# A two-layer transformer kernel: the opening's transform units moved sooner, its fill order rewritten, and several stage joints changed

## The chip, the cores and the metric

The kernel runs on one core of a Trainium2 chip. The metric is the device time of one execution in microseconds (us). The kernel before took 1864.59 us, the median of 3 runs (1861.81 to 1866.3). Engine names are those of the profile: PE is TensorE (PEld are its weight loads), DVE is VectorE, ACT is ScalarE, POOL is GpSimd and SP is SyncE.

## What is computed

The reference is a diffusion transformer of two layers, on 256 tokens of x and 256 tokens of context, model width 2048, branch width 4096. Layer 0 mixes by a two-dimensional Fourier transform in 16 groups of 256 channels; layer 1 is sliding-window attention with a sink and the context as extra keys. Both are modulated by vectors made from c (and c_ctx) by the weights ada_w.

```python
xc = ctx
for i in range(DEPTH):                       # 0: fourier, 1: attention
    shift, scale, gate = split(silu(c) @ ada_w[i] + ada_b[i], 3)
    h = rmsnorm(x, norm_g[i]) * (1 + scale) + shift
    # hc: the same of xc with c_ctx
    if kind == 0:
        u, z = split(h @ w_in, 2)            # 16 groups of 256 channels
        f = fft2(ug, axes=(tokens, channels), norm='ortho').real
        y = einsum('bngc,gcd->bngd', f, w_mix) * silu(z)
        # yc the same of hc
    else:
        q, k, v, z = split(h @ w_in)         # kc, vc from hc
        y = attend_with_sink(q, keys, values, mask) * silu(z)
    x = x + gate * (y @ w_out[i])
    xc = xc + gate_c * (yc @ w_out[i])       # layer 0 only
return rmsnorm(x, final_g)
```

The inputs and the output are float32.

## The kernel before

**Products.** Every large product is made of three matmuls on rounded parts (`mm3`, L74): high by high, high by low, low by high. So each tile has to be split first (`split`, L61): ACT casts the high part, and DVE subtracts it to get the low part. A weight tile arrives as a 1 MB "raw" tile on SP's DMA queue and is split in two halves.

**Order.** A scheduler puts the instructions of each engine in an order, by its own estimate of when they can run. The program steers it with `tc.issue_after(ins)`: what stands in that block comes after `ins`. On the chip each engine, and each queue of DMAs, then works strictly in that order, so one instruction that waits holds all behind it. Buffers come from pools; taking a tile from a full pool waits for the last reader of an old one. [...]

**The opening (L140 to L432).** The modulation weights of layer 0 (shift and scale) are 32 tiles of 1 MB, `in_awp`. `opening_step(p)`, p = 0 to 15, takes two each:

- `ada_tile` (L216) multiplies a weight tile with the conditioning on PE; after eight of them, in two steps, `ada_rows` (L221) copies rows off PSUM on ACT, and `ada_fin` turns them on PE with the identity (L228) and reduces and finishes them on DVE (L232 to L235). Shift (`sh0`) and scale (`gs0`) come in four quarters each.
- `x_split` splits the four token tiles of x for one quarter of the channels, and `dft_unit(k)` applies the token transform to channel block k, 12 matmuls, six for each of the two sequences. `evac_dft` copies the result off PSUM.
- `scale_hx(k)` multiplies by the scale (L288 ACT, L289 DVE), once the scale of that quarter is there. `fix_f0` puts the shift into column 0, the zero frequency (DVE, L239 to L245); it needs the shift of that quarter, so a product that reads column 0 comes after it.
- `fill_pe(n)` takes the next n steps of the list `fill`: the 80 projection steps of groups 0 and 1 (`u_step`: the part "m" reads columns 128 to 255, the part "p" reads columns 0 to 129 and so column 0) and of the special frequencies (`sp_step`, "s", column 0 too). Each step is one `mm3`.
- `uload` says at which step a weight tile of groups 0 and 1 (`in_wu`) is loaded. All loads share a ring of 7 raw slots, later 5 (`raw_st`, L190), and take the slot with the smallest "until".
- `load_m(g)` loads the mixing weights of group g on ACT's queue (one buffer, L354), folds and splits them, and multiplies them with the channel transform on PE (10 matmuls). load_m(0) stands in step 9.

**The groups (L448 to L526).** For each of the 16 groups the two 1 MB weight tiles (halves kh = 0 and 1 of the contraction) are folded into a difference and a sum (`fold_uh`, L132: DVE; for some of them the sum is made in place by an accumulating DMA on POOL's queue, L141), and split into eight tiles (`split_uh`). PE does 48 matmuls of the part "m", then the mix of the group before (14), then 48 of the part "p". The mix writes two tiles of `fd` to DRAM on POOL's queue (L522; the last group's go on ACT's).

**The z stage and the first output product.** Transposed x comes again in tiles `xT` on POOL's queue (L576), is modulated (L582 to L584) and multiplied with `wz`; the result gates `fd`. Then layer 0's output product runs, 32 weight tiles, and `evac0` (L639) adds x, squares on ACT (L645, L648) and adds the squares of the first blocks on DVE (L650).

**The joint to layer 1.** The sums of squares over channels are matmuls with a column of ones (L698, L700). `rsqrt` (L82) makes the norm with POOL's power (L90). Meanwhile `x1_turn` transposes the new x on PE (L690), copies it on ACT (L692), and stores it to DRAM `x1d` on ACT's queue (L693). The norm is broadcast by matmuls (L720) and copied (L721); then `h` of layer 1 is made (L756 to L760) and the key and value product starts, with the first `wkv` tile split before (one half in the last step of the product before, the other while POOL works on the power).

**The tail.** After the attention, `o1_step` multiplies the attention's output, split by `y_split`, with the second half of `w_out[1]`. Channel blocks k under 16 go to the pool `h1`, k = 16 to 19 to `act`, and the others to a pool `ys` that exists only when the attention's own pool is closed.

Of the kernel before, what the change touches and what calls it, by code (L numbers as in the profile page):

```python
# [16 lines left out]
P = 128  # L17
# [5 lines left out]
G = 16  # L23
# [5 lines left out]
def tile_dit(ctx: ExitStack, tc: tile.TileContext, a: dict, out: bass.AP):  # L29
# [29 lines left out]
    last_cast = [None]  # L59

    def split(h, l, src):  # L61
        last_cast[0] = S.copy(h, src).ins  # L62
        V.tensor_tensor(l, src, h.bitcast(F32), op=ALU.subtract)  # L63
# [15 lines left out]
    v_end = [None]  # L79

    def rsqrt(pool, src, w, tag, ahead=None):
# [3 lines left out]
        if ahead is None:  # L85
            V.tensor_scalar(v, src, 1.0 / D, EPS, op0=ALU.mult, op1=ALU.add)
        else:
            V.tensor_scalar(v, ahead, 1.0 / D, EPS, op0=ALU.mult, op1=ALU.add)
            v_end[0] = V.scalar_tensor_tensor(v, src, 1.0 / D, v, op0=ALU.mult, op1=ALU.add).ins
# [53 lines left out]

    def split_uh(v, m):
        fl = {}
        for nm, t in (("m", m), ("p", v)):
            l = wfp.tile([P, 8, 127], F32R, tag="wf", name=f"w{nm}l")
            h = wfp.tile([P, 8, 127], F32R, tag="wf", name=f"w{nm}h")
            split(h, l, t)
            fl[nm] = (h, l)  # L150
        return fl
# [14 lines left out]
    with tc.tile_pool(name="st", reuse_waits="tile", bufs=1, side="right") as st:  # L166
# [22 lines left out]
        def raw_st(src, until):  # L189
            slot = min(ring, key=lambda r: r[1])  # L190
# [58 lines left out]
        def x_split(nb):  # L249
            for s in range(2):  # L250
# [40 lines left out]

        raws, pend = {}, []
        units = {1: (), 2: (4, 5), 3: (6, 7), 4: (8, 9), 5: (10, 11), 6: (12, 13), 7: (14, 15)}

        def opening_step(p):
# [3 lines left out]
            if p in (1, 3, 5):  # L299
                x_split((p + 1) // 2)  # L300
            us_ = units.get(p, ())
            if p < 2:
# [4 lines left out]
            elif us_:  # L307
                for k in us_:
                    dft_unit(k, (0,))
            else:  # L310
                fill_pe(4)
            for i in (2 * p, 2 * p + 1):
                ada_tile(i)
            if p in uload:
                raws[uload[p]] = load_uh(*uload[p], raw_st, uhold[uload[p]])
# [8 lines left out]
            elif p > 7:  # L324
                fill_pe(4)
# [12 lines left out]
        wu = [[None, None], [None, None]]  # L338
        raws[0, 0] = fold_uh(raws[0, 0], 0, 0)
        opening_step(6)  # L340
        with tc.issue_after(rows_end[0]):
            wu[0][0] = split_uh(*raws[0, 0])
        opening_step(7)
        raws[1, 0] = fold_uh(raws[1, 0], 1, 0)
# [32 lines left out]
        ou = [{}, {}]  # L377
        parts = (("m", 128, 256), ("p", 0, 130))

        def u_step(g, nm, k):  # L380
            c0, c1 = dict(m=(128, 256), p=(0, 130))[nm]
            if k == 0:
                ou[g][nm] = psum()[0:127, 0 : 2 * (c1 - c0)].rearrange("p (s j) -> p s j", s=2)
            wh, wl = wu[g][k // 8][nm]
            h, l = hx[k]
            return mm3(ou[g][nm], wh[:, k % 8, :], wl[:, k % 8, :], h[:, :, c0:c1], l[:, :, c0:c1], k == 0, k == KT - 1)

        def sp_step(k):
            if k == 0:
                ou[0]["s"] = psum()[0:32, 0:260].rearrange("p (s j) -> p s j", s=2)  # L390
            h, l = hx[k]
            q = slice(k * 32, (k + 1) * 32)
            return mm3(ou[0]["s"], sph[:, q], spl[:, q], h[:, :, 0:130], l[:, :, 0:130], k == 0, k == KT - 1)
# [8 lines left out]
        def fill_pe(n):  # L402
            for _ in range(n):
                g, nm, k = fill.pop(0)
                with pe_next():
                    r = sp_step(k) if nm == "s" else u_step(g, nm, k)
            pe_end[0] = r

        for p in range(8, 16):
# [9 lines left out]
            if p == 9:  # L419
                with pe_next():  # L420
                    bcast_rows(rr, r_bc)
# [6 lines left out]
            for kh, q in ((0, 9), (1, 11)):  # L428
# [18 lines left out]
    for g in range(G):  # L447
        if g == 2:  # L448
            with tc.issue_after(f0_end[0]):
                w = [split_uh(*f) for f in v2]  # L450
        else:
            w = load_u(g) if g > 1 else wu[g]
# [8 lines left out]
        if g == 1:  # L461
            with tc.issue_after(f0_end[0]):
                pqh, pql, sp = load_m(g)
# [23 lines left out]
        if g == 0:  # L487
            ov = ou[0]["s"]
            S.copy(asp[0:32], ov)
            S.copy(asp[64:96], ov)  # L490
            pqh, pql, sp = m0
            asp_end = V.tensor_tensor(asp[32:64], ov, asp[0:32].bitcast(F32), op=ALU.subtract).ins
# [8 lines left out]
        split(ph, pl, oa["p"])  # L501

        def mix(g=g, mh=mh, ml=ml, ph=ph, pl=pl, pqh=pqh, pql=pql, sp=sp):
            for db in range(2):
# [17 lines left out]
                (nc.gpsimd if g < G - 1 else nc.scalar).dma_start(fd[g * 2 + db], ft.rearrange("p s j -> p (s j)"))  # L522
# [728 lines left out]
```

## Time and profile before

| | |
|---|---|
| runs, median of 3 | 1864.59 us (1861.81 to 1866.3) |
| the profiled execution | 1861.88 us |
| its span | 1859.8 us, so 2.1 us lie around it |
| instructions | 26500 |
| PE busy | 1817.1 us, 98% |
| DVE busy | 1387.8 us, 75% |
| ACT busy | 955.3 us, 51% |
| DMA | 367.42 MB, mean 198 GB/s |

The busy share of an engine is a mean over all stages. The row of forty digits shows the same share for each fortieth of the span, 46.5 us, so the opening is the first two and a half digits. The list of waits names, for one engine, the instruction that waited, what it waited for, the sum of these waits, how often, and the longest. The timeline gives the start and the duration of an instruction (or of several alike in a row, "x16"), and in brackets the idle time of its engine before it and what ended that. A matmul of float32 that is not rounded is shown as two records. "Granted clock" is the share of PE's clock that the chip allowed in that stretch.

### The profile page before, as it was taken

The page shows a single profiled execution, that of the slowest core. Times are in us where ns is not written, and L with a number is a line of the kernel's source. Part 1 is how long each engine was busy: PE and PEld are TensorE (multiplying, and loading weights), DVE is VectorE, ACT ScalarE, POOL GpSimd, SP SyncE. Part 2 cuts the span into 40 slices and gives each one's busy share as a digit, 9 for nine tenths or more (in the row PEclk, how much of TensorE's full clock was granted, in tenths as well). Part 3 has the DMA queues.
Part 4 walks back from the last instruction along what each step waited for, and adds up shares of the span by engine and source line. Part 5 has one row for each costly group of instructions (what it writes and reads, how often), then busy time and mean ns, then how long its engine had stood idle before and what let it go on. Part 6 is the DMA issues. An engine that isn't in the chain of part 4 may idle for free.

```text
span 1859.8 us, 26500 instructions
## 1 busy us (share of the span) xinstructions
PE 1817.1 (98%) x9897; PEld 1549.1 (83%) x9897; DVE 1387.8 (75%) x2770; ACT 955.3 (51%) x1660; POOL 179.4 (10%) x189
## 2 busy tenths in 40 slices
PE   6899999999999999999999999999999999999997
PEld 4579999888888888888888888888888888887886
DVE  4759888786868788588984836888878878887454
ACT  5534445432222243214222524888888888896343
POOL 0011111100000000000000001111220220300001
PEclk9999999999999999999999999999999999999999
DMA  9989888666656547654675324333333333434543
GB/s 394 418 284 246 230 237 238 225 232 231 229 219 232 210 180 271 258 217 149 227 281 218 114 91 144 128 136 125 125 115 135 136 114 136 159 137 178 187 179 136
DMA packets 76129, 367.42 MB, mean 198 GB/s; under 512 B 23200, under 2 KB 23344, under 8 KB 40928
## 3 DMA queue, kind: packets, MB, share of 16 engines
q1 hardware_dynamic: 48960, 324.57, 47.5%
q0 software_dynamic: 22320, 33.15, 7.1%
q10 hardware_dynamic: 4720, 8.00, 1.4%
q8 instruction: 78, 1.28, 0.3%
q14 instruction: 51, 0.42, 0.1%
HBM read 353.10 MB, written 12.59 MB: 197 GB/s over the span
## 4 chain that ended last, share of the span: by engine, by line
PE 79%; DMA 9%; issue 6%; DVE 3%; ACT 2%; POOL 0%; ACTq 0%; SPq 0%; POOLq 0%; DVEq 0%
PE ps L75 19%; PE ps L76 19%; PE ps L77 19%; PE ps L950 6%; PE ps L952 3%; DMA raw<-in_awp 3%; PE ps L1006 3%; DMA raw<-in_wu 3%; PE ps L1021 2%; PE ps L1020 2%; PE ps L986 2%; PE ps L987 2%; PE ps L216 1%; DMA raw<-in_adw 1%; DMA xn<-in_x 1%
## 5 line engine op out<-in xcount | busy, mean ns | idle before, releaser
L62 ACT CAST wh<-raw 128x1024 fp32r<-128x1024 f32 x333 | 349.2, 1051 | 546.3 <-PE ps L76 464.7
L63 DVE TENSOR_TENSOR wl<-raw,wh 128x1024 fp32r<-128x1024 f32 x333 | 421.3, 1267 | 232.0 <-ACT wh L62 229.2
L76 PE MATMUL ps<-act,wh 128*128 128x512 f32 x1024 | 398.2, 389 | 0.0
L75 PE MATMUL ps<-act,wh 128*128 128x512 f32 x1024 | 393.7, 389 | 0.0
L77 PE MATMUL ps<-act,wl 128*128 128x512 f32 x1024 | 392.6, 389 | 0.1
L77 PEld LDWEIGHTS ps<-act,wl 128*128 128x128 f32 x1024 | 192.2, 188 | 40.2 <-DVE wl L63 0.5
L76 PEld LDWEIGHTS ps<-act,wh 128*128 128x128 f32 x1024 | 192.2, 188 | 39.9
L75 PEld LDWEIGHTS ps<-act,wh 128*128 128x128 f32 x1024 | 192.2, 188 | 39.8
L553 DVE CUSTOM_DVE_ANT_0 raw<-raw,cb 128x512 f32<-128x512 f32 x256 | 172.7, 689 | 26.3 <-DMA raw<-in_adw 22.8
L950 PE MATMUL ps<-h,wh 128*128 128x512 f32 x512 | 186.9, 400 | 0.0
L553 DVE CUSTOM_DVE_ANT_0 junk<-raw,cb 128x512 f32<-128x512 f32 x192 | 131.9, 687 | 25.0 <-ACT cb L545 12.5
L952 PE MATMUL ps<-h,wl 128*128 128x256 f32 x512 | 138.1, 280 | 0.0
L75 PE MATMUL ps<-wh,h 128*128 128x512 f32 x320 | 124.1, 396 | 1.6 <-ACT h L757 1.6
L76 PE MATMUL ps<-wl,h 128*128 128x512 f32 x320 | 125.5, 392 | 0.0
L77 PE MATMUL ps<-wh,h 128*128 128x512 f32 x320 | 124.0, 391 | 0.0
L950 PEld LDWEIGHTS ps<-h,wh 128*128 128x128 f32 x512 | 96.1, 188 | 18.8
L988 DVE CUSTOM_DVE_ANT_0 ps<-ps,mask,nsink 128x512 f32<-128x512 f32 x128 | 92.1, 754 | 12.1 <-PE ps L987 11.2
L991 ACT ACTIVATE p<-ps,mx 128x512 f32<-128x512 f32 x128 | 87.3, 687 | 24.7 <-DVE mx L988 24.1
L952 PEld LDWEIGHTS ps<-h,wl 128*128 128x128 f32 x512 | 96.8, 189 | 1.4
L63 DVE TENSOR_TENSOR pl<-ps,ph 128x512 fp32r<-128x512 f32 x128 | 83.7, 685 | 10.0 <-ACT ph L62 8.7
L996 ACT ACTIVATE p<-p,sm 128x512 f32<-128x512 f32 x128 | 85.4, 716 | 8.2 <-DVE sm L994 8.2
L76 PE MATMUL ps<-wl,ys 128*128 128x512 f32 x212 | 83.3, 393 | 0.0
(322 smaller groups left out, 3575.4 us busy)
## 6 DMA issues: line engine op xcount, KB each, us to landing
raw<-in_wz SPq DMA_DIRECT2D x64, 1024.0 KB, 4.9
raw<-in_adw SPq DMA_DIRECT2D x64, 1024.0 KB, 4.9
raw<-in_awp SPq DMA_DIRECT2D x32, 1024.0 KB, 13.0
raw<-in_wo SPq DMA_DIRECT2D x32, 1024.0 KB, 6.1
raw<-in_wq SPq DMA_DIRECT2D x32, 1024.0 KB, 4.8
raw<-in_wu SPq DMA_DIRECT2D x32, 1016.0 KB, 7.0
raw<-in_wo1b SPq DMA_DIRECT2D x16, 1024.0 KB, 4.8
act<-in_xT POOLq DMA_DIRECT2D x32, 256.0 KB, 5.3
```

The lines of the kernel that those rows point to most:

```text
L62: last_cast[0] = S.copy(h, src).ins
L63: V.tensor_tensor(l, src, h.bitcast(F32), op=ALU.subtract)
L75: PE.matmul(o, wh, xh, start=start, stop=False)
L76: PE.matmul(o, wh, xl, start=False, stop=False)
L77: return PE.matmul(o, wl, xh, start=False, stop=stop).ins
L553: V.tensor_tensor_reduce(junk if s == 0 and i < 3 else wf, wf, cb[:, s, kq * 512 : kq * 512 + 512], 1.0, 0.0, ALU.mult, ALU.add, acc[:, i, ...
L950: PE.matmul(o[0], wh[:, q], hx1[k], start=k == 0, stop=k == KT - 1)
L952: PE.matmul(o[0][:, 0:N], wl[:, q], hx1[k][:, 0:N], start=False, stop=False)
L988: V.tensor_tensor_reduce(o, o, mask[:, tb, :], -0.125, nsink[:, i : i + 1], ALU.add, ALU.min, mx[:, tb : tb + 1])
L991: S.activation(pt[:, tb, :], so[tb], AF.Exp, bias=mx[:, tb : tb + 1], scale=-1.0, accum_out=sm[:, tb : tb + 1])
L996: S.activation(pt[:, tb, :], pt[:, tb, :], AF.Copy, scale=sm[:, tb : tb + 1])
L1006: PE.transpose(o[:, (kt * 2 + tb) * P : (kt * 2 + tb + 1) * P], pt[:, tb, c : c + P], ident)
```

## The change

The opening:

- The transform units of blocks 4 to 15 stand in steps 2 to 6 (three, two, three, two, two) instead of two in each of the steps 2 to 7. The x tiles of quarters 2 and 3 are split one sequence at a time, in steps 2, 3, 4.
- Projection steps start in step 7 (eight before the modulation tiles, four after); step 12 has none, step 14 four. The list `fill` goes in runs of four blocks, ordered by the quarter of scale and shift that they need.
- The weight tiles of groups 0 and 1 are loaded in steps 4, 6, 7 and 9 instead of 4, 6, 8 and 10; folds, splits and the closing of the pools move with them.
- The broadcast of the first norm stands in step 5, not after step 9. load_m(1) stands in step 11, not in the loop over groups.

The groups: the m halves of group 2 are split first, and its p halves after the split of group 1's p result. Group 3's loads and splits are to come after the first mix. The `fd` stores of group 14 go on ACT's queue.

The joint: the squares are kept as four sums (blocks 0 to 12, 13, 14, 15). The matmuls that sum the first two stand just ahead of the very last product of the output stage, the other two behind it, and DVE adds the four. The second half of the first `wkv` tile is split after the first `h` is made and the last squares are taken. The x1d stores go on SP's queue.

The tail: y blocks 16 to 23 go to `act`.

```diff
     def split_uh(v, m):
-        fl = {}
-        for nm, t in (("m", m), ("p", v)):
...
+        return {"m": split_part("m", m), "p": split_part("p", v)}
...
-        def raw_st(src, until):
-            slot = min(ring, key=lambda r: r[1])
+        def raw_st(src, until, slots=7):
+            slot = min(ring[:slots], key=lambda r: r[1])
...
-        def x_split(nb):
-            for s in range(2):
+        def x_split(nb, ss_=(0, 1)):
+            for s in ss_:
...
+        fill = []
+        for g, nm, k in ((0, "m", 0), (0, "p", 0), (0, "m", 4), (1, "m", 0), (1, "p", 0), (0, "p", 4), (1, "m", 4), (1, "p", 4), (0, "s", 0), (0, "s", 4), (0, "m", 8), (1, "m", 8), (0, "p", 8), (1, "p", 8), (0, "s", 8), (0, "m", 12), (1, "m", 12), (0, "p", 12), (0, "s", 12), (1, "p", 12)):
+            fill += [(g, nm, k + i) for i in range(4)]
...
-        units = {1: (), 2: (4, 5), 3: (6, 7), 4: (8, 9), 5: (10, 11), 6: (12, 13), 7: (14, 15)}
+        units = {2: (4, 5, 6), 3: (7, 8), 4: (9, 10, 11), 5: (12, 13), 6: (14, 15)}
+        fills = {7: (8, 4), 12: (0, 0), 14: (4, 0)}
...
-            if p in (1, 3, 5):
-                x_split((p + 1) // 2)
+            if p == 1:
+                x_split(1)
+            if p in (2, 4):
+                x_split(p // 2 + 1, (0,))
...
-            else:
-                fill_pe(4)
+            elif fl[0]:
+                fill_pe(fl[0])
+            if p in (3, 4):
+                x_split(p // 2 + 1, (1,))
+            if p == 5:
+                with pe_next():
+                    bcast_rows(rr, r_bc)
...
-            elif p > 7:
-                fill_pe(4)
+            elif p > 6 and fl[1]:
+                fill_pe(fl[1])
...
-        uload = {4: (0, 0), 6: (1, 0), 8: (0, 1), 10: (1, 1)}
-        uhold = {(0, 0): 5.5, (1, 0): 7.5, (0, 1): 8.9, (1, 1): 10.9}
-        for p in range(6):
+        uload = {4: (0, 0), 6: (1, 0), 7: (0, 1), 9: (1, 1)}
+        uhold = {(0, 0): 4.9, (1, 0): 6.9, (0, 1): 7.9, (1, 1): 9.9}
+        for p in range(5):
             opening_step(p)
...
-        fill = [(g, nm, k) for g in range(2) for nm in ("m", "p") for k in range(8)]
-        fill += [(0, "s", k) for k in range(8)]
-        fill += [(g, nm, k) for g in range(2) for nm in ("m", "p") for k in range(8, 12)]
-        fill += [(g, "m", k) for g in range(2) for k in range(12, 16)]
-        fill += [(0, "s", k) for k in range(8, 12)] + [(0, "p", k) for k in range(12, 16)]
-        fill += [(0, "s", k) for k in range(12, 16)] + [(1, "p", k) for k in range(12, 16)]
...
+            if p == 11:
+                with pe_next():
+                    m1 = load_m(1)
-            for kh, q in ((0, 9), (1, 11)):
+            for kh, q in ((0, 8), (1, 10)):
...
         if g == 2:
+            mix0 = ft_end[0]
             with tc.issue_after(f0_end[0]):
-                w = [split_uh(*f) for f in v2]
+                w = [{"m": split_part("m", m)} for v, m in v2]
+                with tc.issue_after(p1_end[0]), tc.issue_after(p1_end[1]):
+                    for f, (v, m) in zip(w, v2):
+                        f["p"] = split_part("p", v)
         else:
-            w = load_u(g) if g > 1 else wu[g]
+            with tc.issue_after(mix0) if g == 3 else nullcontext():
+                w = load_u(g) if g > 1 else wu[g]
...
-                (nc.gpsimd if g < G - 1 else nc.scalar).dma_start(fd[g * 2 + db], ft.rearrange("p s j -> p (s j)"))
+                (nc.gpsimd if g < G - 2 else nc.scalar).dma_start(fd[g * 2 + db], ft.rearrange("p s j -> p (s j)"))
...
-            if 0 < k < 14:
+            if 0 < k < 13:
                 V.tensor_tensor(sqs[0], sqs[0], t2, op=ALU.add)
             else:
                 sqs.append(t2)
 
+        def row_sums(i):
+            for t in range(4):
+                st_end[0] = PE.matmul(sums[0][:, i * 4 + t : i * 4 + t + 1], sqs[i][:, t * P : (t + 1) * P], ones[:, 0:1], start=True, stop=True).ins
...
+                last = i == 31 and (j, b) == (1, 7)
+                if last:
+                    sums.append(psum())
+                    with tc.issue_after(e):
+                        row_sums(0)
+                        row_sums(1)
+                with tc.issue_after(st_end[0]) if last else nullcontext():
+                    e = mm3(o[b], w[j][0][:, q], w[j][1][:, q], *yy[i, j], kg + j == 0, kg * 2 + j == NB - 1)
...
-        nc.scalar.dma_start(x1d[tb, :, c * 512 : (c + 1) * 512], t)
+        nc.sync.dma_start(x1d[tb, :, c * 512 : (c + 1) * 512], t)
...
+    for i in (2, 3):
+        row_sums(i)
+    ssum = const.tile([P, 4], F32, name="ssum")
+    V.tensor_reduce(ssum, sums[0][:, 0:16].rearrange("p (i t) -> p t i", i=4), axis=AX.X, op=ALU.add)
+    r4 = rsqrt(const, ssum, 4, "q")
...
-                with tc.issue_after(h_end[0]):
-                    w = ws_split(raw(a["wkv"][kg])) if kg else w0
+                with tc.issue_after(h_end[0]), tc.issue_after(sq_end[0]):
+                    w = ws_split(raw(a["wkv"][kg])) if kg else [w0, half_split(wr, 1)]
...
-                if 16 <= k < 20:
+                if 16 <= k < 24:
                     t = act(F32R)
...
-                while len(yh) <= min(k + 4, NB - 1) and (len(yh) < 20 or fin):
+                while len(yh) <= min(k + 4, NB - 1) and (len(yh) < 24 or fin):
```

More of the change, by code (lines that the diff above doesn't have):

```diff
@@ L142, in fold_uh, with split_part @@
         return v[:, :, 0, :], m
-    def split_uh(v, m):
-        fl = {}
-        for nm, t in (("m", m), ("p", v)):
[L147 to L151, printed above, removed]
+    def split_part(nm, t):
+        l = wfp.tile([P, 8, 127], F32R, tag="wf", name=f"w{nm}l")
+        h = wfp.tile([P, 8, 127], F32R, tag="wf", name=f"w{nm}h")
+        split(h, l, t)
+        return h, l
+    def split_uh(v, m):
+        return {"m": split_part("m", m), "p": split_part("p", v)}
     def load_u(g):
@@ L298, in opening_step @@
                 x_split(0)
-            if p in (1, 3, 5):
-                x_split((p + 1) // 2)
+            if p == 1:
+                x_split(1)
+            if p in (2, 4):
+                x_split(p // 2 + 1, (0,))
             us_ = units.get(p, ())
+            fl = fills.get(p, (4, 4))
             if p < 2:
@@ L461, in tile_dit @@
         if g == 1:
-            with tc.issue_after(f0_end[0]):
-                pqh, pql, sp = load_m(g)
+            pqh, pql, sp = m1
         elif g > 2:
@@ L489, in tile_dit @@
             S.copy(asp[0:32], ov)
[L490 removed]
+            asp_end = [S.copy(asp[64:96], ov).ins]
             pqh, pql, sp = m0
[L492 removed]
+            asp_end.append(V.tensor_tensor(asp[32:64], ov, asp[0:32].bitcast(F32), op=ALU.subtract).ins)
         mh, ml = am[g % 2]
@@ L692, in x1_turn @@
         S.copy(t, o)
-        nc.scalar.dma_start(x1d[tb, :, c * 512 : (c + 1) * 512], t)
-    sums = [psum(), psum()]
-    for t in range(4):
-        for i in range(2):
-            PE.matmul(sums[0][:, t : t + 1], sqs[i][:, t * P : (t + 1) * P], ones[:, 0:1], start=i == 0, stop=i == 1)
-    for t in range(4):
-        st_end = PE.matmul(sums[1][:, t : t + 1], sqs[2][:, t * P : (t + 1) * P], ones[:, 0:1], start=True, stop=True).ins
-    r4 = rsqrt(const, sums[1][:, 0:4], 4, "q", sums[0][:, 0:4])
-    with tc.issue_after(sq_end[0]), tc.issue_after(v_end[0]):
-        w0.append(half_split(wr, 1))
+        nc.sync.dma_start(x1d[tb, :, c * 512 : (c + 1) * 512], t)
[4 more added lines that the diff above has]
+    r4 = rsqrt(const, ssum, 4, "q")
     r4h = const.tile([P, 4], F32R, name="r4h")
@@ L708, in tile_dit @@
     r_bc1 = act()
-    with tc.issue_after(st_end):
+    with tc.issue_after(st_end[0]):
         o = psum()
```

69 lines of the change are left out of this document (34 added, 35 removed).

## The prediction

> **What bounds the kernel now.** The page first: one busy engine, and it is not full everywhere.
>
> ```profile
> span 1859.8 us, 26500 instructions
> PE 1817.1 (98%) x9897; PEld 1549.1 (83%) x9897; DVE 1387.8 (75%) x2770; ACT 955.3 (51%) x1660; POOL 179.4 (10%) x189
> PE   6899999999999999999999999999999999999997
> DMA  9989888666656547654675324333333333434543
> ```
>
> TensorE is busy for 1817.1 of 1859.8 us. The idle 42.7 us lie in the first slices (the opening), in the tail, and in a few joints. The diff leaves the number of products alone, so it can win only there, or lose by opening new gaps. The list of waits on TensorE says where the gaps are:
>
> ```profile
> PE ps L75 <- DVE dh L184: 12.9, 2, 11.6
> PE ps L216 <- DMA raw<-in_awp: 10.6, 8, 2.9
> PE ps L75 <- ACT h L757: 1.6, 1, 1.6
> PE ps L75 <- ACT mh L62: 1.5, 1, 1.5
> PE ps L76 <- DVE apl L63: 1.3, 1, 1.3
> PE ps L75 <- ACT ys L62: 0.8, 1, 0.8
> ```
>
> The start (12.9 us, for x and the transform) is not touched. The 10.6 us are waits for modulation weights in the opening. The other four are joints, each within reach of a part of the diff. The third view is busy time by stretches of the opening (columns: TensorE, its weight loads, VectorE, ScalarE, GpSimd, granted clock, DMA share, GB/s):
>
> ```profile
> 90.00:100.00 10.00, 7.84 (x64) 5.41 (x62) 5.13 (x16) 2.09 (x2) 0.00 (x0) 1.00 1.01 420
> 100.00:102.00 2.00, 0.98 (x8) 0.33 (x12) 0.00 (x0) 0.00 (x0) 0.00 (x0) 0.59 1.04 434
> 102.00:104.00 2.00, 2.00 (x16) 0.26 (x8) 0.00 (x0) 0.00 (x0) 0.00 (x0) 0.55 0.97 373
> 110.00:120.00 10.00, 9.31 (x67) 6.61 (x66) 7.23 (x24) 5.95 (x16) 3.73 (x3) 1.00 0.68 228
> ```
>
> From 10 to 100 us every window has a DMA share of 1.01 or 1.02 at 416 to 424 GB/s: a 1 MB tile every 2.49 us, and TensorE waits for it. By 110 us this is over, and TensorE is the late one. So the opening is two queues in a row: weights first, then the products that were put off. The timeline at the end of it:
>
> ```profile
> 114.22 2.46 DVE L132 TENSOR_TENSOR wm<-raw 128x1016 f32<-128x1016 f32 x2
> 114.79 1.92 PE L216 MATMUL ps<-raw,c 128*32 128x512 f32 x16
> 118.17 0.60 PE L228 MATMUL ps<-ident,rows 128*128 128x128 f32 x4
> 118.80 0.19 DVE L232 TENSOR_REDUCE sh<-ps 128x8 f32<-128x32 f32 x1 [2.12 <-PE ps L228]
> ```
>
> The last modulation tile landed at 108.56, but TensorE reaches it only at 114.79. That 6.2 us is the slack the opening's rearrangement can use.
>
> **The opening, step by step.** Transform units move from steps 2–7 to 2–6, their x tiles are split in halves, and the products of groups 0 and 1 start at step 7 instead of 8, in an order of what is ready. TensorE's own work is the same but for load_m(1), which moves in from the group loop (10 products, 1.25 us). What changes is when it is done: while weights arrive. load_m(1)'s DMA also comes ahead of the last tiles: 0.26 MB at 0.42 MB/us is 0.6 us, so I put the last landing at 108.56 + 0.6 = 109.2.
>
> Does TensorE keep up? From the tile of step 9 (about 80 us by landings) to step 15's first half I add 28.8 us from rows: 12 products of a projection 1.6, a pair of modulation tiles 1.9, a turned row 0.6, load_m(1) 1.25. So it is there at about 109, with the landing, and done with the last tile at 110.3 instead of 116.71. Behind it come 12 projection products without column 0 (1.6), the turn of the last rows (0.6), 12 more (1.6): 114.1 at most, 113.8 without the ends. Then every product left needs column 0, which is fixed by VectorE after the last rows.
>
> That fix is late next. VectorE has both folds of group 2 ahead of the last reduce in its order, and the second fold needs the second weight tile of group 2. It landed at 115.44; two tiles at 2.49 after 109.2 gives 114.2. Fold 1.21, reduce and fix 1.49 (118.80 to 120.29): 116.9. TensorE stalls about 3.1 us, where before it had no wait at this place. 36 products (4.7) and the first mix (1.75) follow: group 2's m part starts at 123.3, against 127.30.
>
> The stall costs a second time. After 1.86 us idle at 29.14–31.01 the granted clock was 0.53 and 0.62 for 4 us, and 24 products took 4.33 us where others took 3.12. After 2.94 us (98.08–101.02, the lines above) it was 0.59 and 0.55, and 16 weight products took 3.27, not 1.92. After 1.43 to 1.68 us idle it stayed 1.00. The nearest rows to 3.1 say a loss of 1.2; bounds 0 and 1.35 (3.27 − 1.92). Gain of the opening: 4.0 − 1.2 = **2.8 us**. Bounds: 7.6 if the fix costs no stall (the last pair 6.4 sooner, load_m(1) out of the loop 1.25), below nothing if load_m(1) blocks (rival 2).
>
> [...]
>
> **The weights of groups 2 and 3.** Group 2's m halves are split first and its p halves after group 1's. The reason to look: the second m half of group 2 was ready at 130.6 and used at 130.7, that of group 3 at 145.7 for 146.7. If the loop starts 4 us sooner, they must be sooner too. Group 2's was behind the GpSimd accumulate DMAs (126.15 landing, then cast 1.05 and subtract 1.21 of the p half); without that it is ready near 120. Group 3's tile is issued when a raw slot is freed by group 2's split; all that moves 3 us, I get 143 for 144. So the gain is kept, with 1 us to spare. Later groups had 1.1 to 3.4. The wait of 1.26 us at 223.36 hangs on a tile that landed at 219.93 ahead of VectorE's queue (2.33 wait there); its order of folds and splits is the same from there. It goes or stays: **+0.5**, bounds 0 and 1.3.
>
> **Stores of group 14 on ScalarE's queue.** Two issues at 0.33 us on ScalarE; GpSimd's queue can issue xT loads sooner. The 1.55 wait at 333.47 is for a cast behind L583, which waits for L582 and an xT tile that was issued at 323.93, when TensorE freed its buffer, before those stores (325.99). So 0, bounds −0.5 and +0.5.
>
> **Joint of the layers.** The lines before:
>
> ```profile
> 1032.63 1.92 PE L698 MATMUL ps<-ones,act 128*128 128x1 f32 x16 [0.49 <-DVE act L650]
> 1034.41 1.03 PE L700 MATMUL ps<-ones,act 128*128 128x1 f32 x8
> 1039.86 1.25 ACTq L693 DMA_DIRECT2D x1d<-act  x2
> 1041.15 0.59 ACT L721 COPY act<-ps 128x512 f32<-128x512 f32 x1 [0.83 <-PE ps L690]
> 1043.19 0.50 PE L75 MATMUL ps<-wh,h 128*128 128x512 f32 x1 [1.59 <-ACT h L757]
> ```
>
> Row sums are 16 records in 1.92; now there are 32 instead of 24, and 16 stand ahead of the last product. They push its end, the last evacuation and square by about 1.8: sums end at 1033.72 + 1.84 + 1.1 = 1036.7, 1.3 later than 1035.44. One reduce (0.2) is added, one VectorE step (0.16) goes. So r and its broadcast are 1.3 later. Against this, the x1d stores leave ScalarE: the copy at 1041.15 stood behind issues that ended 1041.11 (0.83 idle), and the first h behind one at 1042.25 (0.33): up to 1.0 back. The split of the second weight half leaves VectorE's gap (1.22) and comes behind h, where 24 products (5.5 us) cover it; the raw slot it frees is then some 8 us later, and the next load, before at 1036.80, has until the third tile is used to land. SP's stores wait for ScalarE's copies, and only that load is queued behind them. Sum **−0.3**, bounds −1.3 and +1.0.
>
> **Four more y tiles before the tail.** The casts for the last product wait at 1699.12 stand behind a copy at 1698.84 from the last head. With y 20–23 split early, TensorE has 24 more products (5.6 us) before it needs them. The 0.76 and 0.29 waits go: **+1.0**, bounds 0 and 1.05.
>
> **Sum.** 2.8 + 0.5 + 0 − 0.3 + 1.0 = 4.0 us. The profiled execution took 1861.88 (span 1859.8 and 2.1 around it), 2.7 below the median of 1864.59. So it becomes 1857.9, and the median 1860.6.
>
> **Rivals.**
> 1. *The gain is eaten by supply.* TensorE arrives sooner at groups 2 to 9, but folds and splits are paced by raw slots and VectorE, busy 67.0 of 70 us between 130 and 200. Slacks of 0.1 and 1.0 at the second m halves speak for it, the removed accumulate wait against it. If their times stay, the opening's 2.8 return as waits at L75: 4.0 − 2.8 = 1.2, or 1863.4.
> 2. *Slower: load_m(1) blocks TensorE in the opening.* Its tile has one buffer, so its load is issued only when VectorE has read load_m(0)'s, and VectorE now has two folds, eight scalings and the splits of cst and wsp ahead of that. Such loads took 7.34 and 11.42 us while the DMA was full. TensorE wants it at step 11, about 88 us. Read at 76, as m0's landing at 75.59 allows, it is there at 83 to 88; each microsecond later holds all that follows in order, and the ring with its five slots (12.4 us of transfers) fills up. The stall at the fix hides the first 3.1; beyond it group 2's m part starts at 120.5 + d. Slower by 3.7 needs a loss of 4.9 in the opening, d = 11.6, so VectorE reading m0 at 88 to 92. For it speaks the order, against it that the folds' weights land some two tiles sooner than before. At d = 12: opening −5.2, sum −4.0, 1868.6.
> 3. *No stall at the fix, or no clock drop.* If the second tile of group 2 lands by 111 and TensorE never stalls, the opening gives up to 7.6: sum 8.8, 1855.8. If it stalls and the clock holds, 1859.4. For the first speaks that TensorE frees slots sooner; against it the full DMA.
>    [...]
> 4. *The rearrangement does nothing*: were the opening bound by landings alone. Against it the 6.2 us between 108.56 and 114.79. Joints alone: 1.2, 1863.4, as in 1.
>
> **How the numbers follow.** Forecast 0.43; its own range is 1858.5 to 1862.6 (the joint, the wait of 1.26 and the stores at their ends). Rivals 1 and 4 0.22, rival 2 0.15, rival 3 0.20, half each way. 0.2% is 3.7 us, about what a measurement of this kernel can tell from no change, so faster begins at 1860.9. Of the forecast 0.25 lies below that; with rival 3, 0.45 faster. Same: 0.18 of the forecast and 0.18 of rivals 1 and 4, 0.36. Slower: rival 2 and 0.04 of rival 1 with the joint at its worst, 0.19. The range reaches from just under rival 3's first case to where a third of rival 2 is in, 1855.5 to 1867.5.
>
> **What would show it.** Right: the last modulation pair on TensorE at 109–111; a wait of about 3 us for a fixed column (ScalarE or VectorE f0, L244/L245 before) at 114–117 with a halved clock behind it; group 2's m part at 123–125; no wait for a wml tile until 150; first kv product at 1043.5 less the shift, no issue on ScalarE before the r_bc1 copy; no ys wait near 1699. Wrong: waits for weights of groups 2–4 of over 1 us; the DMA share below 0.9 anywhere from 20 to 100 us; a wait of over 5 us for an mh, cl or spw tile in the opening.

## The result and the profile after

The changed kernel took 1857.84 us, the median of 18 runs (1849.97 to 1861.9), against 1864.3 us for the kernel before (18 runs, 1859.45 to 1867.99): a ratio of 0.9965, 95% interval 0.9955 to 0.9974, so 6.5 us or 0.35% faster. On the chip of the first experiments the same kernel had a ratio of 0.9977 (0.9965 to 0.9988), 4.3 us. Forecast were 4.0 us (1860.6) and a range of 1855.5 to 1867.5.

The profiled execution is the fastest of the 18, 1849.97 us. It is 11.9 us below the profiled execution of before, nearly twice what the medians say. So what is seen in this one profile must not be taken for the effect of the change; the second profiles below sort the two apart.

The page of the changed kernel:

```profile
span 1848.2 us, 26508 instructions
...
PE 1813.5 (98%) x9905; PEld 1548.9 (84%) x9905; DVE 1388.9 (75%) x2769; ACT 955.3 (52%) x1660; POOL 177.2 (10%) x187
```

The list of waits on TensorE:

```profile
PE ps L75 <- DVE dh L182: 12.4, 2, 11.1
PE ps L214 <- DMA raw<-in_awp: 4.8, 5, 2.0
PE ps L75 <- DVE act L242: 2.9, 2, 2.6
...
PE ps L77 <- DVE wml L63: 0.7, 1, 0.7
...
PE ps L75 <- ACT h L776: 0.5, 1, 0.5
...
PE ps L75 <- ACT mh L62: 0.2, 1, 0.2
```

The wait for modulation weights fell from 10.6 to 4.8 us. A new one is there, 2.9 us for L242, the fixed column (2.59 of it at one place, 115.78). Another new one, 0.7 us for wml, stands at 64.72, in the first projection steps. The waits for apl (1.3) and ys (0.8) are gone, those for mh and h are 0.2 and 0.5 instead of 1.5 and 1.6. The end of the opening, in the timeline:

```profile
108.66 1.07 PE L214 MATMUL ps<-raw,c 128*32 128x512 f32 x8 [0.88 <-DMA raw<-in_awp]
...
113.60 1.22 DVE L130 TENSOR_TENSOR wm<-raw 128x1016 f32<-128x1016 f32 x1 [1.25 <-DMA raw<-in_wu]
114.74 0.18 DVE L230 TENSOR_REDUCE sh<-ps 128x8 f32<-128x32 f32 x1
...
115.78 0.39 PE L75 MATMUL ps<-act,wph 128*127 128x260 f32 x1 [2.59 <-DVE act L242]
...
120.51 0.28 PE L75 MATMUL ps<-mh,pqh 127*128 127x256 f32 x1
```

The last tile landed at 108.62 and is multiplied at 108.66. The second fold of group 2 (113.60) stands on VectorE ahead of the reduce (114.74), as read from the order, and TensorE waits 2.59 us. The first mix starts at 120.51 instead of 124.68.

Two profiled executions by place (start of the same instruction in both, us):

| | before | after | difference so far |
|---|---|---|---|
| first mix | 124.68 | 120.51 | −4.2 |
| mix of group 13 | 309.71 | 303.65 | −6.1 |
| mix of group 15 | 333.47 | 326.00 | −7.5 |
| first key and value product | 1043.19 | 1033.60 | −9.6 |
| last product's end | 1849.54 | 1838.09 | −11.5 |

### The profile page after: what moved, and what is told of

Its sections match the earlier page's. It is cut to its first block, busy times and chain, and to the rows that moved or that the text cites. A ratio compares the mean times of both kernels' runs of the same rounds, so it can differ in the third digit from the quotient of the medians.

```text
span 1848.2 us, 26508 instructions
## 1 busy us (share of the span) xinstructions
PE 1813.5 (98%) x9905; PEld 1548.9 (84%) x9905; DVE 1388.9 (75%) x2769; ACT 955.3 (52%) x1660; POOL 177.2 (10%) x187
## 4 chain that ended last, share of the span: by engine, by line
PE 87%; DMA 5%; issue 3%; DVE 3%; ACT 1%; POOL 0%; SPq 0%; POOLq 0%; ACTq 0%; DVEq 0%
PE ps L75 22%; PE ps L76 22%; PE ps L77 22%; PE ps L969 6%; PE ps L971 3%; PE ps L1025 3%; PE ps L1040 2%; PE ps L1039 2%; DMA raw<-in_awp 2%; PE ps L1005 2%; PE ps L1006 2%; DVE raw L565 1%; DMA raw<-in_adw 1%; PE ps L214 1%; DMA raw<-in_wo 1%
## 5 line engine op out<-in xcount | busy, mean ns | idle before, releaser
L969 PE MATMUL ps<-h,wh 128*128 128x512 f32 x512 | 187.2, 400 | 0.0
L75 PE MATMUL ps<-act,wph 128*127 128x260 f32 x256 | 74.2, 290 | 2.9 <-DVE act L242 2.9
```

What stands on the lines that cost most here:

```text
L75: PE.matmul(o, wh, xh, start=start, stop=False)
L969: PE.matmul(o[0], wh[:, q], hx1[k], start=k == 0, stop=k == KT - 1)
```

## The experiments

Waits and times come from each run's own profile, ratios from its timed runs against the kernel before on the same chip.

### Both kernels a second time, and the change in two parts

e1 is the kernel before and e2 the changed one, with no edit. e3 has the first part of the diff above, up to and with `p1_end` (opening and groups), the rest as before; e4 has its second part, from the `fd` line on (stores of group 14, joint, tail), the rest as before.

> The kernel before, unchanged, for a second profile. Two theories of what sets the 11.9 us between the two profiled executions (1861.88 and 1849.97) when the medians differ by 6.5. Place theory: each difference belongs to its place; the profile again has the three stretches of half clock (32 to 35, 100 to 104 and 1036 to 1039 us) and the waits of 1.3 us for apl near 223 and 1.5 us for mh near 333, and its time is within 1 us of 1862. Chance theory: stretches of half clock come and go between executions, so at least one of the three is missing or another is there, and the time differs by 1.7 us for each; the waits for apl and mh stay within 0.3 us of before.

> The changed kernel, unchanged, for a second profile. Place theory: no half clock at the joint near 1028, one stretch near 70 to 74, time near 1850. Chance theory: more stretches of half clock than the one of the first profile, and a time nearer the median of 1857.8. Both: a wait of 2.6 us for the fixed column near 113 to 116, group 2's m part at 122.5 to 124 us, no wait for apl near 217.

> The opening and the group order of the change, with the stores of group 14, the joint and the tail as before. Place theory: group 2's m part at 122.5 to 124 us, the wait for apl of 1.3 us gone (both belong to this part), so 4.2 + 1.4 = 5.6 us faster than before; the wait for mh near 327 is 1.5 us as before if the stores of group 14 removed it, and gone if the earlier groups did. Rival (supply): the opening's gain is given back by waits for weights in groups 2 to 9: under 2 us.

> The stores of group 14, the joint and the tail of the change, with the opening and groups as before. Place theory: 1.5 (mh) + 1.8 (joint of the layers) + 1.9 (tail) = 5.2 us faster than before. My prediction: 0 - 0.3 + 1.0 = 0.7 us. If the joint's gain is the clock alone, and chance, between 1.5 and 4 us by times, with the tail's 1.0 to 1.9 sure.

Measured: e1 1863.92 us, ratio 1.0007 (0.9992 to 1.0022); e2 1858.08, 0.9977 (0.9965 to 0.9988); e3 1859.52, 0.9983 (0.9971 to 0.9994); e4 1860.68, 0.9981 (0.9965 to 0.9996). So the halves are worth 3.2 and 3.5 us, together 6.7, and the whole 4.3 (2.2 to 6.5): the intervals are too wide to say whether they add. For e3 that is 1.1 to 5.4 us: the 5.6 of the place theory is just outside, a part of the supply theory's under 2 is inside. For e4 it is 0.7 to 6.5 us, which holds both the 5.2 and the 0.7: the time alone decides nothing there, and the profile has to.

The second profile of the changed kernel took 1861.01 us, 11 us more than the first. Its list of waits:

```profile
PE ps L76 <- DVE apl L63: 4.1, 6, 1.9
PE ps L75 <- DVE act L242: 3.2, 2, 2.6
...
PE ps L75 <- ACT mh L62: 1.0, 1, 1.0
```

The opening is the same, but there are six waits for apl, in mixes of groups 3 to 10, that the first profile has not. The longest, in the timeline of e2:

```profile
188.76 1.22 DVE L130 TENSOR_TENSOR wm<-raw 128x1016 f32<-128x1016 f32 x1 [3.48 <-DMA raw<-in_wu]
...
190.56 1.21 DVE L63 TENSOR_TENSOR wpl<-raw,wph 128x1016 fp32r<-128x1016 f32 x1
...
191.69 0.42 DVE L63 TENSOR_TENSOR apl<-ps,aph 127x260 fp32r<-127x260 f32 x1
...
192.16 0.39 PE L76 MATMUL ps<-apl,pqh 127*128 127x260 f32 x1 [1.94 <-DVE apl L63]
```

VectorE waits 3.48 us for a weight tile (issued when its slot came free at 181.28, landed 188.73), and apl stands behind. wpl stands there too, and its subtract is what frees the next slot, so one late load makes the next one late. In the first profile the corresponding load was issued at 177.25 and VectorE waited 1.73. From the first mix to that of group 13 it took 183.1 us in the first profile and 188.5 in the second; e1 and before 184.8 and 185.0. The opening's gain of 2.6 us in e2 (first mix at 122.07 against 124.67 in e1) was a loss of 1.1 by group 13. e3 shows the same (188.7, waits for apl 4.6 us): by group 13 its profile is 1.4 us behind e1, so the 3.2 us of its timed runs are not to be seen there.

Also different is the granted clock. The windows of e2 behind the stall and at the joint:

```profile
114.00:116.00 2.00, 0.00 (x0) 0.00 (x0) 1.86 (x6) 0.72 (x1) 1.07 (x2) 1.00 0.90 337
116.00:118.00 2.00, 1.84 (x8) 1.71 (x9) 1.98 (x10) 1.23 (x7) 1.18 (x1) 0.50 1.28 159
118.00:120.00 2.00, 2.00 (x14) 1.92 (x13) 2.00 (x5) 0.62 (x1) 0.00 (x0) 0.65 1.42 178
...
1038.00:1040.00 2.00, 2.00 (x11) 2.00 (x12) 0.56 (x4) 1.02 (x3) 1.32 (x2) 0.50 0.00 0
```

and the same stretches of the first profile of the changed kernel:

```profile
116.00:118.00 2.00, 2.00 (x16) 1.77 (x15) 1.98 (x10) 0.86 (x6) 0.81 (x1) 1.00 1.35 167
118.00:120.00 2.00, 2.00 (x18) 1.92 (x17) 2.00 (x5) 1.15 (x3) 0.00 (x0) 1.00 1.35 168
...
1028.00:1030.00 2.00, 2.00 (x21) 2.00 (x21) 0.51 (x4) 1.82 (x5) 1.27 (x2) 1.00 0.00 0
```

In e2 the granted clock is 0.50 behind the 2.6 us stall and in the joint's transposes, in the first profile 1.00 at both. The program is the same in both, so the clock at these two places is decided by the execution, as the chance theory has it. In the kernel before all three stretches came again in e1 (32 to 35, 100 to 104, 1036 to 1043 us; by the clock of the windows 3.4, 3.4 and 6.8 us long); but e4, with the same opening, has a clock of 1.00 at 32.

The joint can be sorted by it. From the hundredth-last record of the output product to the first key and value product, us:

| stretches of half clock in it | old joint | new joint |
|---|---|---|
| none | 32.1 (e3) | 32.1 (after), 32.1 (e5) |
| one | 33.9 (before), 33.1 (e9) | 33.3 (e2, e6, e10) |
| two | 35.0 (e1) | 34.8 (e4), 34.8 (e11), 34.6 (e12) |

At the same number of stretches the new joint is between 0.3 us longer and 0.6 us shorter. The 1.8 us by which the two first profiles differ here are one stretch of half clock.

The tail is not chance: from the first key and value product to the end it took 804.2 to 804.5 us in the ten profiles with the four more y tiles, and 806.3 to 806.5 in the four without (before, e1, e3, e9): 2 us.

### What holds the groups: slots or VectorE

e5 gives the weight tiles of groups 3 to 15 a fourth raw slot. Room for it is made by single buffers in load_m (one of the two is shown) and by another pool for `cst`:

```diff
+    def raw4(src):
+        turn[0] += 1
+        if turn[0] % 4:
+            return raw(src)
+        t = ru.tile([P, D], F32, tag="raw4", name="raw4")
+        nc.sync.dma_start(t[:, : src.shape[-1]], src)
+        return t
...
-            lr = ua.tile([P, 2, GD], F32R, tag="ml", name="ml")
+            lr = ua.tile([P, 2, GD], F32R, tag="ml", name="ml", bufs=1)
```

> The changed kernel with a fourth raw slot for the weight tiles of groups 3 to 15 (room for it is made by single buffers for the split of w_mix). Supply theory: the waits for apl (4.1 us in six in the second profile of the changed kernel, 4.6 in the one with the opening alone) come from the cycle of the three raw slots: a slot is held over its load, its fold, the accumulating DMA of 11 to 12 us and the split. With a fourth they are gone, the stretch from the first mix to that of group 13 takes 183 us instead of 188.5, and the kernel gains 3 to 5 us on the changed one. Rival (VectorE): VectorE, 67 of 70 us busy there, is what paces the groups; then a fourth slot changes nothing, the waits for apl stay at 4 us and the time at 1858.

Measured: 1853.43 us (7 runs, 1852.49 to 1854.77), ratio 0.9951 (0.9933 to 0.9969): some 4.7 us less than the changed kernel in e2, at 7 runs with a spread of 2.3 us. e2 ran on another chip; on this one e7 and e8 below, which differ from the changed kernel only in the row sums, took 1859.0. Its waits:

```profile
PE ps L214 <- DMA raw<-in_awp: 5.3, 5, 2.0
PE ps L75 <- DVE act L242: 2.9, 2, 2.6
...
PE ps L77 <- DVE wml L63: 0.8, 1, 0.8
```

No wait for apl is left in the list. First mix at 122.20, with half clock behind the stall as in e2 (0.84, 0.50 and 0.81 in the windows from 116 to 122); to that of group 13 it took 183.1 us, as in the best profile of the changed kernel. VectorE has the same work, so the amount of it was not what paced the groups. The accumulating DMAs took 9.1 us in the mean here, 11.8 in e2, 10.8 in the first profile and 10.2 before. The edit also changes the scheduler's order on VectorE, so a part of the effect can be that order; the slots alone were not tried without it.

e9 makes the same edit in the kernel before.

> The kernel before with the fourth raw slot of the earlier run. Supply theory: the kernel before loses some 2 us to the three slots in groups 2 to 13 (from the mix of group 1 to that of group 13 it took 175.9 to 176.1 us, and 173.7 to 174.1 where no product waits), so 1.5 to 3 us faster than before, 1859.5 or so, waits for apl under 0.3 us. The opening's gain is then the difference between the changed kernel with four slots and this one: 2.5 (opening) + 1.9 (tail) = 4.4 us. Rival: the fourth slot itself brings what the earlier run gained (0.9951), then this one is at 1855 or below.

Measured: 1866.23 us, ratio 1.0025 (1.0013 to 1.0037), slower, where 1.5 to 3 us less were expected. The run is inconclusive on the whole: the edit moved VectorE's order so that the mix of group 0 waits 6.1 us for asp. Behind that place it bears the theory out: from the mix of group 1 to that of group 13 174.5 us instead of 176.1 (before) and 175.9 (e1), with no wait for apl in the list. The kernel before lost about 1.5 us there.

### The stall at the fixed column

e6 brings the last reduce and the fix ahead of the second fold:

```diff
-            v2 = [fold_uh(v2[kh], 2, kh) for kh in range(2)]
+            v2[0] = fold_uh(v2[0], 2, 0)
         with tc.issue_after(fold_end[0]):
             ada_fin(*pend.pop())
         fix_f0(3)
+        with tc.issue_after(f0_end[0]):
+            v2[1] = fold_uh(v2[1], 2, 1)
```

> The changed kernel with the last shift's reduce and the fix of column 0 ahead of the second fold of group 2. Both theories: the stall of 2.6 us before the first column-0 product shrinks to under 0.5, no half clock at 116 to 120, and the first mix starts at 118 to 119.5 us instead of 120.5 to 122. Path theory: the kernel gains 2.4 to 4 us on the changed one. Supply theory: the groups give it back, so under 1 us.

Measured: 1853.47 us (6 runs, 1851.61 to 1854.84), ratio 0.9948 (0.9928 to 0.9967). The first mix starts at 119.14. The timeline at the two places where TensorE needs a fixed column:

```profile
74.83 0.39 PE L75 MATMUL ps<-act,wph 128*127 128x260 f32 x1 [1.74 <-DVE act L242]
...
114.13 0.79 DVE L242 CAST act<-f 128x2 fp32r<-128x2 f32 x4
114.35 0.39 PE L75 MATMUL ps<-act,wph 128*127 128x260 f32 x1
...
116.22 1.21 DVE L130 TENSOR_TENSOR wm<-raw 128x1016 f32<-128x1016 f32 x1
```

The stall is gone, as expected: the fix (114.13) now stands ahead of the second fold (116.22), and the product at 114.35 has no idle time of note before it. The list still has 1.7 us for L242, but that is the fix of the first quarter, at 74.83, where the first profile waited 0.35. The clock was 1.00 at 116 to 120; two other stretches of half clock came, at 75.1 and at 122.9, behind 1.7 and 1.8 us of idle time (the second for asp, in the mix). No wait for apl is in the list; from the mix of group 1 to that of group 13 it took 173.7 us, against 179.6 in e2. The supply theory, by which the groups would give the gain back, is wrong here: the new order keeps them supplied with three slots (accumulating DMAs 10.8 us). The gain is 5.5 us on e7 and e8, more than the 2.4 to 4 of the path theory; the waits for apl, which went too, fit the rest. So another order does without a fourth slot what e5 does with one, and the number of slots alone does not decide.

e10 has the edits of e5 and e6. e11 also puts the split of group 2's second m half behind asp:

```diff
-                w = [{"m": split_part("m", m)} for v, m in v2]
+                w = [{"m": split_part("m", v2[0][1])}]
+                with tc.issue_after(asp_end[1]):
+                    w.append({"m": split_part("m", v2[1][1])})
```

> The changed kernel with the fourth slot and with the fix of column 0 ahead of the second fold of group 2. Supply theory: with the slots free, the earlier start of the groups (first mix at 119.1 instead of 122.2, less a wait of 1.8 us for asp in it) is kept to the end: 1 to 3 us faster than either alone, 1851 to 1852.5. Rival: both removed the same waits for apl, so their gains do not add and the time stays at 1853.5.

> As the run with both, and the second m half of group 2 is split after asp on VectorE, so the first mix does not wait 1.8 us for asp. By places: wait for asp under 0.8 us, 1 us faster than both; second m half of group 2 ready near 124 for a use near 126, so no new wait. If VectorE's order only moves the wait to another tile, the same time as both.

Measured: e10 1852.86 us, ratio 0.995 (0.9933 to 0.9968); e11 1852.75 (6 runs, 1852.49 to 1853.2), 0.9948 (0.9931 to 0.9966). The gains of the two edits do not add, which is what the rival said: the first mix starts at 118.22 and 118.89, 3 to 4 us ahead of e5, and by the mix of group 13 all four are at 304.5 to 305.3 us. In e11 the wait for asp fell to 1.0, and a wait of 1.9 us for mh of load_m at 138 took its place. The lead of e10 on e5 shrinks by 3.6 us between the two places. Its waits there are 1.8 us for asp and, near 189, 0.8 for apl and 0.3 for ft, in all 2.9 against 0.4 in e5; so 2.5 of the 3.6 are waits, and the slow start of the products behind them makes some 0.5 more, an estimate from the tail below, where two waits of together 1.05 us cost 1.5. Four versions (e5, e6, e10, e11) are 0.5% faster than the kernel before and 0.25 to 0.3% faster than the changed one; they are not told apart by these runs.

e12 leaves the stall and gives TensorE work in it:

```diff
+        fill_pe(4)
+        spare = psum()[:, 0:256].rearrange("p (s j) -> p s j", s=2)
+        for _ in range(7):
+            with pe_next():
+                r = mm3(spare[0:32], sph[:, 0:32], spl[:, 0:32], hx[0][0][:, :, 128:256], hx[0][1][:, :, 128:256], True, True)
+            pe_end[0] = r
         fill_pe(len(fill))
```

> The changed kernel with 21 extra products, whose result is not used, on TensorE in the stall before the first column-0 product (2.5 us at 0.12 each; nothing is left out). Clock theory: five of six profiles of this stall showed half clock behind it because TensorE had nothing to do; with work there is no half clock at 114 to 122 us and the first mix starts near 120.7 us, as in the one profile without it, instead of 121.6 to 122.4. Rival: half clock comes from something else in that stretch and appears all the same. Supply theory: the 1.2 us do not reach the end, unless the scheduler's new order of VectorE, which this edit also brings in groups 2 to 8, changes the waits for apl; those are read from the same profile.

Measured: 1859.57 us, ratio 0.9977 (0.9961 to 0.9992). The windows of e12:

```profile
114.00:116.00 2.00, 1.80 (x16) 1.46 (x15) 1.86 (x10) 1.01 (x2) 1.06 (x2) 1.00 0.92 290
116.00:118.00 2.00, 2.00 (x15) 1.79 (x16) 1.98 (x9) 0.94 (x7) 0.89 (x1) 1.00 1.32 163
118.00:120.00 2.00, 2.00 (x19) 1.91 (x18) 2.00 (x5) 1.00 (x2) 0.00 (x0) 1.00 1.44 179
```

The clock stays at 1.00 and the first mix starts at 120.57, as expected. One profile is not proof where one of six without filler had a full clock too. The 1.5 us do not reach the end: seven waits for apl (2.2 us), 187.2 us to the mix of group 13, and a time as that of the changed kernel.

### The row sums

e7 puts all four row sums behind the last product, e8 makes each 32 columns wide:

```diff
 e7
-                    with tc.issue_after(e):
-                        row_sums(0)
-                        row_sums(1)
...
-    for i in (2, 3):
+    for i in range(4):
 e8
-ones[:, 0:1], start=True
+ones[:, 0:1].broadcast_to([P, 32]), start=True
```

> The changed kernel with all four row sums behind the last product of the output stage. Theory that columns one wide do not keep the clock up: 32 records in a row (3.8 us) bring half clock for the transposes every time, so 20 transposes take 3.5 to 4.5 us as in the three profiles with half clock, not 2.34. Theory of chance: as with the sums ahead, none, one or two stretches. The order alone: sums end 0.8 us later with them behind than ahead, if the squares of the last block are in time; from the hundredth record before the joint to the first key and value product 32.1 us with full clock, 33.3 with one stretch, 34.8 with two.

> The changed kernel with each row sum done for 32 equal columns in place of one. Theory that narrow columns let the clock drop: the sums take at most 0.3 us longer in all, and the clock stays at 1.00 through the joint. [...]

Measured: e7 1859.02 us, ratio 0.9979 (0.9967 to 0.9992); e8 1859.04, 0.9979 (0.9967 to 0.9992). Neither differs from the changed kernel (e2 0.9977). In e7, with 32 narrow records in a row, the clock was 1.00 in every window from 1024 to 1046, so narrow columns do not bring half clock every time, and the theory of narrow columns falls. e8 had a full clock too, which then says nothing. The stretch of the joint took 32.4 us in e7 and 32.9 in e8, 32.1 in the changed kernel at full clock. Both lists have a wait of 0.9 us for r4h (0.2 in the first profile).

## Why the prediction was right, point by point

**The opening: right.** I put the last modulation tile at 109.2 and done at 110.3, a stall of 3.1 us, the first mix 2.8 us sooner with half clock behind the stall and 4.0 without. Measured: landing 108.62, done 109.73, stall 2.59 (2.6 in all six profiles that have it), and the first mix 2.3 to 3.1 us sooner with half clock (e2, e3, e5, e7, e8, against before) and 4.2 without (the first profile). Both cases of the sum occurred, with the one I took as the likelier. load_m(1) held up nothing that shows (its tile landed at 79.67): rival 2 did not happen. Two readings were loose. The row at 114.79 is of the last two tiles; the last one was reached at 115.67, so the slack was 7.1 us and not 6.2. And load_m(1)'s transfer, to which I gave 0.6 us, came ahead of the last tiles before the change, too (issued at 76.84). A sign that I had excluded did come, the wait of 0.7 us for a wml tile at 64.72; it is small.

**The groups: wrong.** The step that failed is "So the gain is kept, with 1 us to spare", with +0.5 for the wait at 223. I looked at the slack of the m halves only. These were in fact early (second m half of group 2 ready at 119.5 for 126.2, of group 3 at 139.2 for 142.1 in the first profile). What comes late is apl, behind a fold that waits for its tile. I had seen that very wait at 223.36 and taken it for a single event. Rival 1 named the mechanism, raw slots, and priced it as the loss of the gain. The runs showed both ends: no loss in the first profile (1.9 us gained from the first mix to group 13's), 3.5 to 4.5 us lost in e2, e3, e7 and e8. So four of the five profiles with this opening and order lost more than the opening had gained. In which share of the executions without a profile it happens can't be seen from the runs. What tips it is open: the profile that kept its supply had the earliest first mix of the five (120.51), so an earlier start alone does not explain it, and the change also orders the splits and loads of groups 2 and 3 anew, which no run undoes by itself.

**Stores of group 14: right at nothing.** The wait for mh was 0.2 in the first profile, 1.0 in e2 and 1.3 in e4, which have the edit, and 1.5, 1.5 and 0.6 in before, e1 and e3, which have not. It varies as much within as between.

**The joint: right in the sum (−0.3, bounds −1.3 and +1.0).** At the same clock it is worth between −0.3 and +0.6 us. The sums were indeed later, but by less: from the start of the last three records, or of the sums in their place, to the first transpose it took 4.12 us before (1031.29 to 1035.41) and 4.71 after (1023.48 to 1028.19), 0.6 more where I had 1.3. And the copy of r_bc1 no longer waits for DMA issues: it starts 0.1 us after the last broadcast product (1031.80, 1031.90), not 0.9 (1040.27, 1041.15), and h is waited for 0.5 us instead of 1.6. The half clock was not in my sum at all, and it is the larger part: up to 2.7 us between two profiles of the same joint.

**The tail: right in its cause, too small.** The waits for ys are gone in all profiles with the edit. I took 1.0, the two waits added, with 1.05 as the most. It is 2: the two gaps cost 1.5 us counted from start to start, since the products behind an idle time start 0.34 us apart instead of 0.23, and some of the later ones ran at 0.24 instead of 0.23.

**The total.** −4.0 forecast, −4.3 and −6.5 measured. In the second pair of profiles, 2.8 us apart, the opening's 2.6 us were gone by group 13 (−3.7 in the groups); what remains is the tail (2.0) and one stretch of half clock less at the joint (1.6). The clock does not make the difference of the medians: its mean over the timed runs is 0.9956 in e2 and 0.9957 in the kernel before on that chip. So the total is right because a term of up to −4 in some executions (supply) and the undersized tail (+1) stand against each other, with the clock either way in single executions. That is luck in part. The bound of rival 3, 1855.8, is near the versions without waits for apl (1853), but in e5 the stall, whose absence was rival 3's reason, is still there.

**The clock.** Behind 2.6 us of idle time half clock came in five of six profiles and not in one, behind 2.0 us near 70 in seven of ten. In e6 and e11 it came only behind a second idle time of 1.7 and 1.8 us near 75, in e12 at neither place (1.6 us there). In e9 it came behind 1.4 us (at 61 and at 75), where the same 1.4 us near 61 left the clock at 1.00 in before and e1. So no one length of idle time tells the cases apart here, and the outcome changes between executions of the same order, as in e2 and the first profile.

## What to carry to other kernels

Where an engine's order holds both the unit that frees a buffer and a unit that waits for the next load into one, read the slack of everything behind that load, not only of the tile that is loaded: here one late load made the next one late (VectorE waited 3.48 us for it in e2, 1.73 in the first profile), the same program kept its supply in one execution and not in another (183.1 and 188.5 us to the mix of group 13), and a fourth buffer or another order gave some 0.25% on top of the change. A sum of waits counts the idle time only; the slow restart (in the tail 0.34 us from start to start instead of 0.23), and the half clock, which here came behind 2.0 us of idle time in seven of ten profiles, behind 2.6 us in five of six, and behind 1.4 to 1.8 us in e6, e9 and e11, are to be added. Take a second profile of both kernels before explaining a difference of a few microseconds.

## What was not expected of the hardware

- Up to the last product, the stretches of half clock in these profiles were 3.36 to 3.44 us long by the clock of the windows, or 6.84 (at the joint of e1, for one), and whether an idle time of 1.4 to 2.6 us brought one changed between profiles: 2.6 us did in e2 and not in the first profile of the same program, 1.4 us near 61 did in e9 and not in before and e1. Of 18 runs of the changed kernel the six with a mean granted clock of 0.997 took 1854.3 us in the mean, the three with 0.994 1859.3. 0.003 of 1850 us is 5.5 us, about the difference. But the six alone spread over 8.9 us, and half clock behind the last product, where no product is left to slow down (5.9 us in the first profile, from 1842 on, the last product ending at 1838.09), counts in the mean as well, so how much of a run's time is the clock is not shown.
- An accumulating DMA of 0.5 MB took 10.2 us in the mean in the groups of the kernel before and 10.8 in the first profile, at most 13.3 and 13.1, where a plain load of 1 MB took 6.6 and 6.8 in the mean. Over the profiles it was longest where apl was waited for (9.1 us with none in e5, 11.8 with 4.1 us in e2 and 4.7 in e7, 12.4 with 2.2 in e12); which of the two is the cause was not tried.
